# Row-wise infinity norm: early stores released one reduction sooner, and five load semaphores instead of eight

## The chip, the cores and the metric

The kernel runs on one core of a Trainium2 chip. The metric is the device time of one execution in microseconds (us); the median of several executions is quoted. The time span of a profile starts with the first instruction and is about 1.8 us shorter than the device time of the same execution. A DMA is a transfer between memory and the core; its landing is the moment when the last of its 16 completion signals has arrived, and "issue to landing" counts from the start of the instruction that issues it. A semaphore is a counter that those signals raise and that an engine can wait for.

## The reference

```python
def setup_inputs():
    return {"x": np.random.randn(8192, 8192).astype(np.float32)}

def reference(x):
    return np.linalg.norm(x, ord=np.inf, axis=1)      # max |x| of each row
```

The input is 268 MB and the output 32 KB, so nearly all of the work is to read the input once.

## The kernel before

SyncE issues all loads into a ring of three big buffers, and VectorE (DVE) reduces each piece with an absolute maximum. Most rows go in 24 loads of 16384 columns per partition, the first of the tail included. The tail (18 rows per partition) is cut into 29 pieces that get shorter towards the end, so that little is left to reduce when the last one lands. Load i may not go out before the reduction of load i-SEMS has ended, because it uses the same semaphore:

```python
SEMS = 8
...
    def load(self, at, w, src):
        i = self.started
        self.started += 1
        ins = self.nc.sync.dma_start(out=self.ring[:, at : at + w], in_=src)
        ins.then_inc(self.sems[i % SEMS], 16)
        ...
        if i >= SEMS:
            self.tc.add_manual_dep(ins.ins, self.last[i - SEMS].name, ...,
                reason="the semaphore counts one load at a time")
    def reduce(self, pairs):
        ...
        self.last.append(ins.ins)
```

The results go out in three stores: `early` (all rows of the big loads) and `middle` (16 of the 18 tail rows) from ScalarE, and `last` (the final two rows) from SyncE. The first two carry an added wait:

```python
    early = nc.scalar.dma_start(out=out[:split]..., in_=res_big...)
    middle = nc.scalar.dma_start(out=out_tail[:, : ROWS - 2], in_=res_tail[:, : ROWS - 2])
    for store in (early, middle):
        tc.add_manual_dep(store.ins, pieces.last[-2].name, ..., reason="not beside the last load")
    ...
    last = nc.sync.dma_start(out=out_tail[:, ROWS - 2 :], in_=res_tail[:, ROWS - 2 :])
```

## Time and profile before

| | before |
|---|---|
| device time, median (range) of 4 runs | 629.31 us (629.28 to 629.45) |
| span of the profile | 627.7 us |
| DVE busy | 552.1 us, 88% |
| DVE idle from 560 us to its end | none |
| last load, issue to landing | 8.85 us |
| end of DVE's work, then to the end of the span | 625.14 us, 2.54 us |

What sets the time in each stretch is worked out, with the lines, in the prediction. It was made when three of these four runs were at hand, with a median of 629.32 us.

### The profile page before, as it was taken

How to read it: one execution, taken by the hardware profiler on the slowest of the kernel's cores; microseconds unless marked ns; L12 is line 12 of the kernel's file. 1: busy time of each engine (PE TensorE's matmuls, PEld its weight loads, DVE VectorE, ACT ScalarE, POOL GpSimd, SP SyncE). 2: the span in 40 equal slices, each digit the busy share in tenths (PEclk: the TensorE clock that was granted, in tenths of full speed). 3: DMA queues.
4: the chain of work that ended last, by engine and by line, in shares of the span. 5: the costliest groups of instructions: out<-in, count | busy, mean ns of one | idle time of the engine just before them, and what ended most of it. 6: DMA issues, size and time to landing. Idle time of an engine off the chain costs nothing.

```text
span 627.7 us, 175 instructions
## 1 busy us (share of the span) xinstructions
DVE 552.1 (88%) x62; POOL 3.2 (1%) x14
## 2 busy tenths in 40 slices
DVE  0588988889988889888898888988889999999998
POOL 0000000000000000000000000000000000000000
DMA  9999999999999999999999999999999999999997
GB/s 401 405 464 405 464 405 464 405 464 401 468 401 468 401 468 401 468 401 468 401 464 405 464 405 459 409 459 409 451 407 442 425 420 438 430 434 429 423 421 296
DMA packets 7921, 268.48 MB, mean 428 GB/s; under 512 B 1264, under 2 KB 1264, under 8 KB 2416
## 3 DMA queue, kind: packets, MB, share of 16 engines
q1 hardware_dynamic: 7632, 268.44, 99.3%
q10 hardware_dynamic: 288, 0.03, 0.0%
q14 instruction: 1, 0.01, 0.0%
HBM read 268.44 MB, written 0.03 MB: 428 GB/s over the span
## 4 chain that ended last, share of the span: by engine, by line
DMA 57%; DVE 42%; issue 0%; DVEq 0%; SPq 0%
DMA ring<-in_x_dram 57%; DVE res_big L110 22%; DVE parts L110 12%; DVE res_tail L110 7%; DVE ring L110 1%; DVEq L265 0%; SPq L92 0%; DVE idle L218 0%
## 5 line engine op out<-in xcount | busy, mean ns | idle before, releaser
L110 DVE TENSOR_REDUCE res_big<-ring 128x2 f32<-128x16384 f32 x23 | 396.1, 17220 | 69.7 <-DMA ring<-in_x_dram 69.7
L110 DVE TENSOR_REDUCE parts<-ring 128x1 f32<-128x3136 f32 (+18 forms) x22 | 78.5, 3633 | 1.2 <-DMA ring<-in_x_dram 1.2
L110 DVE TENSOR_REDUCE res_tail<-ring 128x1 f32<-128x8192 f32 (+1 forms) x9 | 69.8, 7811 | 2.1 <-DMA ring<-in_x_dram 2.1
L110 DVE TENSOR_REDUCE ring<-ring 128x1 f32<-128x1600 f32 (+5 forms) x6 | 8.3, 1444 | 0.0
L207 POOL TENSOR_SCALAR res_tail<-parts 128x1 f32<-128x1 f32 x9 | 2.7, 298 | 615.9 <-DVE parts L110 615.9
L207 POOL TENSOR_SCALAR parts<-parts 128x1 f32<-128x1 f32 x1 | 0.4, 357 | 5.6 <-DVE parts L110 5.6
L254 POOL MEMSET const-uint8-127<- 128x1 uint8 x1 | 0.1, 103 | 0.0
L254 POOL MEMSET const-bfloat16-1.0<- 128x1 bf16 x1 | 0.1, 102 | 0.0
L254 POOL MEMSET const-float32-0.0<- 128x1 f32 x1 | 0.1, 99 | 0.2 <-issue 0.2
L254 POOL MEMSET const-float32-1.0<- 128x1 f32 x1 | 0.1, 99 | 0.0
L218 DVE MEMSET idle<- 1x1 f32 x2 | 0.1, 59 | 0.0
## 6 DMA issues: line engine op xcount, KB each, us to landing
ring<-in_x_dram SPq DMA_DIRECT2D x3, 4096.0 KB, 40.5
ring<-in_x_dram SPq DMA_DIRECT2D x1, 7264.0 KB, 31.1
ring<-in_x_dram SPq DMA_DIRECT2D x1, 5024.0 KB, 33.3
ring<-in_x_dram SPq DMA_DIRECT2D x1, 4544.0 KB, 34.5
ring<-in_x_dram SPq DMA_DIRECT2D x1, 4224.0 KB, 40.3
ring<-in_x_dram SPq DMA_DIRECT2D x1, 4032.0 KB, 35.5
ring<-in_x_dram SPq DMA_DIRECT2D x1, 3584.0 KB, 43.6
ring<-in_x_dram SPq DMA_DIRECT2D x2, 1568.0 KB, 39.0
```

The costliest lines, as they stand in the source:

```text
L110: ins = self.nc.vector.tensor_reduce(out=dst, in_=src, axis=mybir.AxisListType.X, op=mybir.AluOpType.max, apply_absolute_value=True,)
L207: combined = nc.gpsimd.tensor_scalar(out=to, in0=best, scalar1=two[0], scalar2=two[1] if len(two) == 2 else None, op0=mybir.AluOpType.max, ...
L218: tc.keep_in_program_order(nc.vector.memset(idle[:, i : i + 1], 0.0))
L254: nc = _bacc.Bacc("TRN2", target_bir_lowering=False, num_devices=1)
```

## The change

The intent, as the code shows it: let the early stores get out of the last store's way, without running beside the last load, and make do with fewer semaphores.

```diff
-SEMS = 8
+SEMS = 5
...
     for store in (early, middle):
         tc.add_manual_dep(
             store.ins,
-            pieces.last[-2].name,
+            pieces.last[-3].name,
```

No instruction is added or removed.

## The prediction

> **What bounds the kernel now.** I read the page first, then busy time by stage, then the chain that ended last, then the timeline of the end and the list of DMA issues. The kernel loads 268 MB and takes the largest absolute value of each row on VectorE (DVE). By stage (columns: window, its length, DVE busy, POOL busy, clock, DMA share, GB/s):
>
> ```profile
> 0.00:465.00 465.00, 395.27 (x23) 0.19 (x4) 1.00 1.00 433
> 465.00:560.00 95.00, 91.66 (x15) 0.56 (x2) 1.00 0.99 427
> 560.00:615.00 55.00, 55.00 (x16) 2.12 (x7) 1.00 1.00 424
> 615.00:625.10 10.10, 10.10 (x11) 0.36 (x1) 1.00 0.83 333
> 625.10:627.70 2.60, 0.04 (x3) 0.00 (x0) 1.00 0.11 13
> ```
>
> Up to 465 us the DMA engines are full (share 1.00, 433 GB/s) and DVE has spare time: the load bounds. From 560 us to 625.1 us DVE has no idle time at all, and the DMA engines are full too, to about 623 us: the pieces of the tail are cut so that each lands just ahead of its reduction. After 625.1 us there are 2.6 us in which only the last results are stored. The chain says the same of the end:
>
> ```profile
> 618.62 4.86 DVE ring L110 x4
> 623.48 0.06 DVE parts L110
> 623.53 0.69 issue
> 624.22 0.92 DVEq L265
> 625.14 0.00 DVE idle L218 x2
> ```
>
> It is DVE's work without a gap until 625.14 us. The timeline of the end (start, length, engine, line):
>
> ```profile
> 624.25 0.89 DVE L110 TENSOR_REDUCE res_tail<-ring 128x1 f32<-128x710 f32 x1
> 624.37 0.38 ACTq L220 DMA_DIRECT2D out_dram<-res_big  x1
> 624.51 0.36 POOL L207 TENSOR_SCALAR res_tail<-parts 128x1 f32<-128x1 f32 x1 [10.81 <-DVE parts L110]
> 624.79 0.51 ACTq L224 DMA_DIRECT2D out_dram<-res_tail  x1
> 625.08 0.06 DVE L218 MEMSET idle<- 1x1 f32 x2
> 625.16 0.35 SPq L239 DMA_DIRECT2D out_dram<-res_tail  x1
> ```
>
> The two early stores go out at 624.37 and 624.79 us, the last store at 625.16 us. The list of issues gives size and time from issue to landing:
>
> ```profile
> ring<-in_x_dram SPq DMA_DIRECT2D x1, 384.0 KB, 10.1
> ring<-in_x_dram SPq DMA_DIRECT2D x1, 352.0 KB, 8.9
> out_dram<-res_big ACTq DMA_DIRECT2D x1, 23.0 KB, 2.1
> out_dram<-res_tail ACTq DMA_DIRECT2D x1, 8.0 KB, 1.8
> out_dram<-res_tail SPq DMA_DIRECT2D x1, 1.0 KB, 1.7
> ```
>
> So the stores land at about 626.4, 626.6 and 626.8 us, the last store last, and some 0.85 us of closing instructions follow to 627.7 us. The last load was issued 8.9 us before it landed: it stood in the queue most of that time.
>
> **What the Trainium skill says.** (1) "DMA: Bandwidth & Descriptors", section "Anatomy of one DMA": a semaphore wait is made on the issuing sequencer before dispatch, and the DMA engines only consume their queues. The trace agrees: SyncE's own waits are all on reductions (456.2, 81.6 and 58.7 us for the three groups on line 92). The section also says that the fixed cost of a DMA is mostly completion latency; 1.7 us for a store of 1 KB fits. (2) Same page, "Why a DMA increments its semaphore by 16 and not by 1": one semaphore for each slot in flight. That is what SEMS is here: load i may not be issued before load i-SEMS has been reduced. (3) Same page, "Issuing engines are not separate DMA queues": DMAs of ScalarE and SyncE interleave on the same 16 engines, so early stores can get in the way of a load or of the last store. (4) "Perfetto Trace Analysis", section "Per-instruction lifecycle": descriptor generation is shared and locked for one DMA at a time. The second early store occupies 624.79 to 625.30 us, and the last store begins at 625.16 us inside that time, yet its own issue takes 0.35 us against 0.33 us of an undisturbed load issue. So at most 0.02 us of such waiting shows in the issue itself.
>
> **The change, part one: five semaphores.** It adds and removes no instruction; 52 loads and their reductions stay. What moves is the earliest issue of a load.
>
> In the first 465 us nothing moves: the ring holds three buffers of 16384 columns, so load i waits for reduction i-3 already, which is stricter than i-5. In the tail the pieces shrink (from 9088 columns to 704), more than five fit into the ring, and the wait becomes reduction i-5 in place of i-8. I worked out the tail's piece list from the kernel's planning function: the last eight pieces, loads 44 to 51, have 1600, 1472, 1344, 1152, 1024, 896, 768 and 704 columns.
>
> The last load, number 51, is the tightest. Before, it waited for reduction 43 and was issued at 615.33 us. After, it waits for reduction 46, the one of 1344 columns. That starts at 618.54 us and takes 1.55 us (list of groups by shape), so it ends at 620.10 us and the issue comes at about 620.12 us: 4.8 us later. Is that late? It needs a figure for a load that finds the queue empty. The first load of the kernel does: issued at 0.72 us, DVE released at 22.9 us, 22.1 us for 8 MiB, while consecutive loads of that size that stand in the queue land 19.3 us apart. So 22.1 - 19.3 = 2.8 us is the fixed part, as an estimate, and a cold one. The 352 KB at the 434 GB/s that 19.3 us means take 0.83 us. Even with an empty queue it would land at 620.12 + 2.8 + 0.83 = 623.75 us, and it landed at 615.33 + 8.85 = 624.18 us before. Spare time: 0.4 us. So there is still a queue ahead of it and it lands when it did.
>
> The load before it, number 50 (384 KB): reduction 45 ends at 618.62 us, so 618.64 + 2.8 + 0.91 = 622.35 us against 613.27 + 10.06 = 623.33 us; spare 1.0 us. Load 49 (448 KB): reduction 44 ends at 617.03 us, so 617.05 + 2.8 + 1.06 = 620.9 us against 610.94 + 11.42 = 622.36 us; spare 1.5 us. Farther back the pieces are larger and the spare time grows: load 40 could be issued when reduction 35 ends, 590.0 us, and landed at 605.1 us. Expected cost of part one: 0.0 us. It also gains nothing: DVE is the bound there, and a queue that is less deep moves no more bytes.
>
> **Part two: the early stores wait for the last reduction but two.** They waited for the reduction of load 50, which ends at 624.34 us (768 columns, start 623.39 us, 0.945 us); now for that of load 49 (896 columns, start 622.40 us, 1.076 us), which ends at 623.48 us. Both stores move up by 0.86 us: issues at 623.51 and 623.93 us, landings at about 625.6 and 625.8 us in place of 626.4 and 626.6 us. The last load has nearly all its bytes by then: the DMA share is 0.97 for 622 to 623 us and 0.29 for 623 to 624 us, and by the trace its last data packet ends at 623.73 us, while the first packet of an early store comes 0.88 us after its issue, thus at about 624.4 us. So the stores still do not run beside the load.
>
> What it can gain: the end is set by the last store, whose issue waits for DVE at 625.14 us, which does not move. Only its 1.67 us from issue to landing can shrink, by what the two early stores disturb it. In the trace its first packets (626.01 us) follow straight on the last packets of the second early store (626.00 us), so some disturbance is possible; but its first packet comes 0.84 us after its issue, which is no more than the 0.88 us of the first early store, which nothing disturbed. I take 0.1 us as the gain, out of a possible 0 to 0.3 us.
>
> **Sum.** 629.32 - 0.0 - 0.1 = 629.2 us.
>
> **Rivals.** (a) The queue runs dry. If the fixed part of an issue near the end is over 3.2 us in place of 2.8 us, load 51 lands late, and each 0.1 us of lateness is 0.1 us of time, because its reduction starts only 0.07 us after its landing now (624.25 against 624.18 us). In favour: 0.4 us is not much, and the 16 DMA engines do not finish together, so the fastest could run dry first. Against: first packets of the very first load came 1.0 to 1.8 us after its issue, and load 51's packets began at 621.9 us, 1.8 us after the new issue. It would give 629.5 to 630.3 us. (b) The early stores meet the last load after all. They are 31 KB together, less than 0.1 us at the rate of the loads, and small packets could make it 0.3 us; 629.3 to 629.6 us. Against: the 0.65 us between the load's last packet and the store's first. (c) The early stores were the real hold-up of the last store, through the shared descriptor generation or their writes in HBM: without them 1.67 us becomes 1.3 us and the time 628.9 us. Against: the 0.84 us above. (d) A shorter queue makes the loads themselves quicker or slower in the tail. Quicker gives nothing, since DVE has no gap there; slower would show at once. The DMA share of 1.00 in both long stages gives no reason for either.
>
> **Range and chances.** The three runs before spread by 0.17 us, and another chip or run may add as much. With (c) at the low side and (a) or (b) at the high side, 628.8 to 629.7 us should hold 8 times in 10; I give (a) one chance in ten. Two per cent would be 12.6 us; no part touches the first 465 us, and the whole end after DVE is 2.6 us. Faster 0.01, within 2% 0.98, slower 0.01.
>
> **What would show it.** Right: the early stores issue near 623.5 and 623.9 us, the last store still at 625.16 us with 1.5 to 1.7 us to landing; the last load has about 4.1 us from issue to landing in place of 8.9 us, and load 50 about 4.7 us in place of 10.1 us; DVE has no idle time from 560 us on. Wrong: a wait of DVE for the DMA of the ring near the end, or a last store that lands in under 1.4 us, or DVE's end away from 625.14 us by over 0.2 us.

## The result, and the profile after

| | before | after |
|---|---|---|
| device time, median of 4 runs | 629.31 us | 629.03 us |
| range | 629.28 to 629.45 | 628.94 to 629.06 |
| ratio | | 0.9996 (0.9981 to 1.0011) |

The ratios are from the runs of the same rounds; they can differ by up to 0.0003 from the ratio of the medians or of the means given here. The medians differ by 0.28 us, and in these eight runs the ranges do not overlap, but the stated interval includes 1.

Busy time by stage in the changed kernel (columns as in the prediction):

```profile
560.00:615.00 55.00, 55.00 (x16) 2.11 (x7) 1.00 1.00 423
615.00:624.95 9.95, 9.95 (x11) 0.36 (x1) 1.00 0.86 338
624.95:627.30 2.35, 0.03 (x3) 0.00 (x0) 1.00 0.04 1
```

DVE still has no gap from 560 us on, with five semaphores too. The stretch after DVE is shorter. The end of the changed kernel's timeline (start, length, engine, line):

```profile
623.35 0.38 ACTq L220 DMA_DIRECT2D out_dram<-res_big  x1
623.77 0.45 ACTq L224 DMA_DIRECT2D out_dram<-res_tail  x1
624.09 0.88 DVE L110 TENSOR_REDUCE res_tail<-ring 128x1 f32<-128x710 f32 x1
...
624.92 0.06 DVE L218 MEMSET idle<- 1x1 f32 x2
625.00 0.35 SPq L239 DMA_DIRECT2D out_dram<-res_tail  x1
```

The two early stores now go out 1.0 us earlier, before the last reduction starts in place of after it. The list of DMA issues of the changed kernel (size, then us from issue to landing):

```profile
ring<-in_x_dram SPq DMA_DIRECT2D x1, 384.0 KB, 4.7
ring<-in_x_dram SPq DMA_DIRECT2D x1, 352.0 KB, 4.1
out_dram<-res_big ACTq DMA_DIRECT2D x1, 23.0 KB, 1.7
out_dram<-res_tail ACTq DMA_DIRECT2D x1, 8.0 KB, 2.4
out_dram<-res_tail SPq DMA_DIRECT2D x1, 1.0 KB, 1.5
```

The last load is issued 4.1 us before it lands instead of 8.9 us, yet it lands 0.85 us after the load before it in both profiles (623.33 to 624.18 us before, 623.19 to 624.04 us after). The last store takes 1.47 us instead of 1.67 us.

The span fell by 0.39 us (627.68 to 627.29 us). The traces divide it: 0.16 us lies at the very start, where the first load landed at 22.68 us instead of 22.85 us and everything after it moved along; 0.20 us lies in the last store; 0.03 us lies in the closing instructions. In the groups of waits this start is the "longest" column of DVE's waits on the big loads (total, times, longest), first before, then after:

```profile
DVE res_big L110 <- DMA ring<-in_x_dram: 69.7, 23, 22.9
```

```profile
DVE res_big L110 <- DMA ring<-in_x_dram: 69.6, 23, 22.7
```

Nothing in the change touches the first load. So one pair of profiles cannot say whether 0.39, 0.20 or 0.0 us belongs to the change; the experiments had to.

### The profile page after: what moved, and what is told of

The parts are those of the page before. It is cut to its first block, busy times and chain, and to the rows that moved or that the text cites. A ratio compares the mean times of both kernels' runs of the same rounds, so it can differ in the third digit from the quotient of the medians.

```text
span 627.3 us, 175 instructions
## 1 busy us (share of the span) xinstructions
DVE 552.1 (88%) x62; POOL 3.2 (1%) x14
## 4 chain that ended last, share of the span: by engine, by line
DMA 57%; DVE 42%; issue 0%; DVEq 0%; SPq 0%
DMA ring<-in_x_dram 57%; DVE res_big L110 22%; DVE parts L110 12%; DVE res_tail L110 7%; DVE ring L110 1%; DVEq L265 0%; SPq L92 0%; DVE idle L218 0%
```

## The experiments

The theories were: **A**, the early stores had disturbed the last store, and moving them away gives the gain; **B**, the five semaphores give it; **C**, it is scatter between executions. (The expectation of stores_latest calls something else theory C: that stores do not disturb one another.) All runs of this section were on the same chip, each group with runs of the kernel before in its rounds. The medians of before were 629.28, 629.30 and 629.31 us in the three groups. Every kernel gave a correct result.

### The two parts apart

**after_again**: the changed kernel once more, no edit.

> The changed kernel once more. Theory A (the early stores disturbed the last store): 0.15 to 0.3 us faster than before, the last store 1.4 to 1.55 us from issue to landing. The first load's landing, which was 0.17 us earlier in the one profile of after (22.68 against 22.85 us), need not repeat, if it is chance of one execution. Theory C (all of the 0.28 us is scatter between executions): within 0.1 us of before.

Measured: 628.97 us (628.90 to 629.25, 5 runs) against 629.28 us; ratio 0.9995. The gain repeats, so theory C alone is unlikely. But its profiled execution, at 629.25 us the slowest of the five, had a last store of 1.87 us, outside the expected 1.4 to 1.55 us: two of the store's 16 completions came 0.3 us after the others. So getting the stores apart does not make the last one quick every time.

**sems5_only**:

```diff
-SEMS = 8
+SEMS = 5
```

> Five semaphores alone, early stores as before. Theory A: 0.0 us against before (within 0.1), last load about 4.1 us from issue to landing, DVE without idle time in the tail, last store again 1.6 to 1.7 us to landing. Theory B (the shorter queue or the fewer semaphores bring the gain, for instance by an earlier first landing): 0.15 to 0.3 us faster, first landing near 22.68 us.

Measured: 629.15 us (629.12 to 629.50, 5 runs); ratio 0.9999. By the means it is 0.06 us faster than before. The list of issues of this kernel:

```profile
ring<-in_x_dram SPq DMA_DIRECT2D x1, 352.0 KB, 4.1
...
out_dram<-res_tail SPq DMA_DIRECT2D x1, 1.0 KB, 2.0
```

The last load goes out as late as in the changed kernel and the last store is as slow as in the kernel before, or slower (1.99 us, above the expected 1.6 to 1.7 us). Its first landing was early too (22.49 us), and yet the time did not fall by the 0.15 us or more of theory B.

**stores_only**:

```diff
-            pieces.last[-2].name,
+            pieces.last[-3].name,
```

> Early stores one reduction earlier alone, eight semaphores. Theory A: all of the gain, 0.15 to 0.3 us faster than before, last store 1.4 to 1.55 us to landing. Theory B: within 0.1 us of before.

Measured: 629.06 us (628.93 to 629.47, 5 runs); ratio 0.9997; by the means 0.20 us faster than before. In its list of issues the last load is early again (8.9 us) and the last store quick:

```profile
ring<-in_x_dram SPq DMA_DIRECT2D x1, 352.0 KB, 8.9
...
out_dram<-res_tail SPq DMA_DIRECT2D x1, 1.0 KB, 1.4
```

This is what theory A said, but 0.20 us against a scatter of 0.2 us between single runs (standard deviation, before and here) called for a second test, below.

### How near the queue is to running dry

**sems4**:

```diff
-SEMS = 5
+SEMS = 4
```

> The changed kernel with four semaphores: the last load waits for reduction 47, at about 621.3 us, in place of reduction 46. If the fixed part of an issue with an empty queue is 2.8 us, as the first load gave it, the last load lands at about 624.9 us, and the kernel is 0.7 us slower than after, with waits of about 0.4 us before each of the last two reductions. With 2.4 us: 0.3 us slower, one wait. With 3.2 us: 1.1 us slower, three waits. If the queue never runs dry: no change.

Measured: 629.97 us (629.64 to 630.23, 5 runs), by the means 0.93 us slower than after_again in the same rounds. The profiled execution was the fastest of the five. Its timeline shows two waits of DVE, and its chain of the end now runs through the last load:

```profile
622.49 1.09 DVE L110 TENSOR_REDUCE ring<-ring 128x1 f32<-128x896 f32 x1 [0.23 <-DMA ring<-in_x_dram]
...
623.82 0.95 DVE L110 TENSOR_REDUCE parts<-ring 128x1 f32<-128x768 f32 x1 [0.24 <-DMA ring<-in_x_dram]
```

```profile
621.16 3.50 DMA ring<-in_x_dram
624.66 0.02 issue
624.69 0.89 DVE res_tail L110
```

The last load took 3.50 us from issue to landing. Less 0.83 us for its bytes, that leaves 2.67 us as its fixed part; the two loads before it, for which DVE waited, leave 2.97 and 2.98 us. That is close to the 2.8 us that the prediction took from the first load. The queue was not quite empty, though: the first packet of the last load came at 622.67 us, and packets of the load before it ran until 623.49 us. There were two waits, as expected at 2.8 us, but they came one load earlier than expected (before the reductions of loads 49 and 50) and were 0.23 and 0.24 us long in place of 0.4 us. One semaphore fewer and the tail is bound by the loads.

**sems3**:

```diff
-SEMS = 5
+SEMS = 3
```

> The changed kernel with three semaphores. The chain of load, reduction, next load closes: with a fixed part of 2.8 us the model gives the last landing at 628.1 us, 4.0 us slower than after, with DVE waiting before each of the last eight loads by 0.4 to 0.9 us; with 2.4 us 2.8 us slower; with 3.2 us 5.3 us slower.

Measured: 635.78 us (634.4 to 637.1, 4 runs); ratio to before 1.0103. That is 6.5 us slower than before by the means, more than the 4.0 us at the expected fixed part, and its runs scatter over 2.7 us. Eight reductions waited, as expected, by 0.32 to 1.06 us, but they were not the last eight: those of loads 42, 43, 45 and 47 to 51. The fixed parts of the last four loads, worked out as above, were 2.5 to 3.0 us. Loads 43 to 45, whose bytes also queue behind a load still in flight, took 3.8 to 4.5 us beyond their own transfer, which the simple model left out. The direction held, the place in part; the size was too small.

### Where the early stores may stand

**stores_latest** (both early stores wait for the last reduction):

```diff
-            pieces.last[-3].name,
+            pieces.last[-1].name,
```

> Five semaphores, both early stores wait for the last reduction itself, so that all three stores go out together near 625.0 to 625.4 us. Theory A: the stores are in each other's way, the later of them lands at 627.2 to 627.5 us, and the kernel is 0.7 to 1.0 us slower than after; the last store itself takes over 1.6 us. If stores do not disturb one another (theory C), the last store still takes about 1.5 us and only the second early store, issued some 0.4 us later, sets the end: 0.3 to 0.6 us slower than after.

Measured: 629.49 us (629.41 to 629.79, 5 runs) against 629.30 us before; some 0.5 us slower than the changed kernel of the other groups. That is the size named if stores do not disturb one another, and theory A's numbers were missed. Its timeline:

```profile
624.74 0.35 SPq L239 DMA_DIRECT2D out_dram<-res_tail  x1
624.74 0.39 ACTq L220 DMA_DIRECT2D out_dram<-res_big  x1
625.17 0.45 ACTq L224 DMA_DIRECT2D out_dram<-res_tail  x1
```

The store of the last rows went out at the same time as the first early store and was not slowed (1.49 us); the two early stores took 1.66 and 1.64 us, and the second one, issued last, set the end. Neither of these is slow: the first early store took 1.69 to 2.19 us in the five profiles with the stores one reduction earlier, and the second one 1.58 to 2.76 us in all nine profiles in which it went out at the end. So stores that start together need not slow one another, and theory A must be narrowed: it can hold only for a last store that comes behind others. In this one look the last store had none ahead of it.

**stores_m6** (the stores go out beside the last four loads):

```diff
-            pieces.last[-3].name,
+            pieces.last[-6].name,
```

> Five semaphores, both early stores wait for the last reduction but five, so that they go out near 619.9 and 620.3 us, beside the last four loads. The comment in the kernel says that this is to be avoided. If their 256 small packets and their writes hold up the loads (rival b of the prediction): a wait of DVE of 0.1 to 0.4 us for one of loads 48 to 51, and 0.1 to 0.4 us slower than after. If not: as fast as after within 0.1 us, since the last store is as much alone as there.

Measured: 629.15 us (628.91 to 629.26, 5 runs) against 629.30 us. Its timeline shows the price that the kernel's comment fears:

```profile
624.30 0.89 DVE L110 TENSOR_REDUCE res_tail<-ring 128x1 f32<-128x710 f32 x1 [0.17 <-DMA ring<-in_x_dram]
```

The last load took 4.36 us instead of 4.08 us and DVE waited 0.17 us for it. But the last store, now alone, took 1.44 us, so the kernel is not slower than before. By the means it is 0.07 us slower than after_again of the other group, less than the 0.1 us expected and within the scatter. So rival (b) is real in the trace, and its cost in time does not show.

**stores_free** (no added wait):

```diff
-    for store in (early, middle):
-        tc.add_manual_dep(
-            store.ins,
-            pieces.last[-3].name,
...
```

> Five semaphores, no added wait on the early stores: each goes out when its data is there, the first near 466 us, the second near 608 us, beside loads that have deep queues. Theory A: the last store is alone, as in after, 1.4 to 1.55 us to landing; the time is that of after within 0.1 us, unless a load in the stretch near 608 us is held up by more than its spare time of under 0.2 us before DVE, then 0.1 to 0.4 us slower.

Measured: 629.08 us (628.93 to 629.35, 5 runs); ratio 0.9997. The stores take 16.2 and 6.2 us among the loads without a gap on DVE in the tail, and the last store takes 1.44 us. By the means it is 0.07 us from after_again, as expected.

### Both factors again, in the same rounds

These four kernels are the corners of a square: stores as before or free, eight or five semaphores. The edits are those of sems5_only and stores_free, alone or together, on the kernel before.

> The kernel before against itself: ratio 1.000 within 0.0003; it measures the scatter. In its profile the first load's landing, 22.85 us in the one profile of before but 22.34 to 22.68 us in the nine others, should fall among those if it is chance of an execution; near 22.85 us if it belongs to the kernel before. The last store should again take 1.6 to 2.0 us, with its 16 completions spread over 0.4 us or more.

> Five semaphores alone, a second time. Theory A: within 0.1 us of before and of before_again. Theory B: 0.15 us or more faster than both.

> Eight semaphores, no added wait on the early stores, so that the last store is alone. Theory A: 0.2 to 0.3 us faster than before, last store near 1.44 us to landing, equal to free5_again within 0.1 us. Theory B: less gain than free5_again by 0.1 us or more.

> Five semaphores, no added wait on the early stores, a second time. Theory A: 0.2 to 0.3 us faster than before, last store near 1.44 us to landing, equal to free8.

| mean time, us (runs) | eight semaphores | five semaphores |
|---|---|---|
| stores as before | 629.21 (5) | 629.22 (4) |
| stores free | 629.06 (6) | 628.98 (5) |

The ten runs of before in these rounds had a mean of 629.28 us, so the same kernel under two names differs by 0.07 us: that is the scatter. The ratio of before_again rounds to 1.0000, as expected. Freeing the stores gains 0.15 and 0.23 us between the corners. Five semaphores change 0.0 and 0.08 us, which is about the scatter, though 0.08 us is near the 0.1 us that theory B asked for. In the profile of before_again the last store's 16 completions spread over 0.40 us, also as expected. The expected "within 0.1 us" held for sems5_again against both before and before_again. The gain of free8 over before_again, 0.15 us, is that over before, 0.22 us, less the scatter just named. The list of issues of free8 has the last store alone:

```profile
out_dram<-res_big ACTq DMA_DIRECT2D x1, 23.0 KB, 16.2
out_dram<-res_tail ACTq DMA_DIRECT2D x1, 8.0 KB, 6.2
out_dram<-res_tail SPq DMA_DIRECT2D x1, 1.0 KB, 1.4
```

The profiles put together, by what stood near the last store:

| profile | first landing | DVE's end to end of span | last store, issue to landing |
|---|---|---|---|
| before | 22.85 us | 2.54 us | 1.67 us |
| before_again | 22.48 us | 2.51 us | 1.65 us |
| sems5_only | 22.49 us | 2.83 us | 1.99 us |
| sems5_again | 22.47 us | 2.73 us | 1.46 us |
| after | 22.68 us | 2.31 us | 1.47 us |
| after_again | 22.48 us | 2.71 us | 1.87 us |
| stores_only | 22.57 us | 2.29 us | 1.43 us |
| stores_free | 22.40 us | 2.28 us | 1.44 us |
| free8 | 22.51 us | 2.31 us | 1.45 us |
| free5_again | 22.57 us | 2.30 us | 1.46 us |

The stretch after DVE has a mean of 2.65 us in the first four profiles (stores close), 2.44 us in the next three (stores one reduction earlier), and 2.30 us in the last three (stores long gone). Of the profiles that the table leaves out, sems4 and sems3 also have the stores one reduction earlier, with 2.28 and 2.26 us (the mean of that kind is then 2.37 us), and stores_m6 has them gone, with 2.28 us. In sems5_again the last store was quick, but the early store ahead of it took 2.2 us and landed 0.36 us after it, and so it set the end. A finer measure separates the kinds without exception: the median of the last store's 16 completions came 1.37 to 1.73 us after its issue in the four profiles with the stores close, and 1.31 to 1.32 us after it in all nine with the stores one reduction earlier or more. after_again is among the nine; two late completions alone made its 1.87 us. With the stores close, the packets of the second early store ended within 0.03 us of the last store's first packet, or ran beside its packets; in the nine they had ended 0.4 us or more before.

The first landing, by contrast, moves within both kinds: the 22.85 us of the first profile of before did not come again.

## Why the prediction was right

The time of 629.03 us fell inside the range, and "within 2%" was right. That says little: the range of 0.9 us also holds the unchanged kernel. The steps are the test:

- **Five semaphores cost 0.0 us.** Confirmed. The last two loads took 4.08 and 4.71 us from issue to landing (forecast: about 4.1 and 4.7 us), DVE had no gap in the tail, and sems5_only and sems5_again stayed with the repeated before. The spare time was put at 0.4 us from a fixed part of 2.8 us; sems4 measured 2.67 to 2.98 us, which by the same sum makes the spare time about 0.25 to 0.55 us, and lost 0.93 us, where 0.7 us was expected. Rival (a) was the right danger, one semaphore farther on.
- **The early stores move and do not meet the load.** Confirmed. They issued at 623.35 and 623.77 us; with the 0.16 us by which this whole execution ran earlier, these are the forecast 623.51 and 623.93 us. The first store packet, at 624.23 us, came 0.63 us after the last packet of the load. stores_m6 shows rival (b) where it does occur: 0.17 us of DVE's wait, which the quicker last store paid for.
- **A gain of 0.1 us.** The mechanism was right and the size was low. The prediction looked at the time from the last store's issue to its first packet, 0.84 us, and took that it was undisturbed. It was: it stayed at 0.85 us after the change. What shrank came after the last packet: from there to the landing it was 0.62 us before and 0.42 us after. The term measures about 0.2 us in the mean: 0.20 us in stores_only, 0.15 and 0.23 us in the square, 0.21 us in the stretch after DVE. Rival (c), in a smaller form than the 0.3 to 0.4 us named, was part of the truth. The 1.47 us in the profile of after lie just under the 1.5 to 1.7 us that were named as the sign of being right.
- **The rest of the 0.28 us** is not settled. A part of up to 0.09 us could belong to the semaphores: with the stores alike, five were faster than eight by 0.06 (sems5_only against before), 0.09 (after_again against stores_only), 0.0 and 0.08 us (the square). The same kernel differed from itself by 0.07 us, so this cannot be told from scatter. The earlier first landing in the profile of after is chance of an execution: it ranges from 22.40 to 22.85 us over the table, more than the change is worth, so a part of the first 0.28 us may be luck.

Why a store close behind another sometimes completes late was not found. It is no fixed cost: in sems5_again the last store landed after 1.46 us with close neighbours. And a landing can be late without neighbours so close, by a few of the 16 completions, as in after_again.

No kernel tried beats the changed one: free5_again, with 628.99 us against its 628.97 and 629.03 us, is the same.

## What to carry to other kernels

Where an engine works without a gap up to the end, as DVE here, a deeper load queue gained nothing that could be measured. How shallow it may get can be worked out: the issue time under the new wait, plus the fixed part of a load that finds the queue empty, plus its bytes, must lie before its old landing. After the last reduction only the last store counts, so send the other results out before it, by as much as the loads allow. Effects of 0.2 us in 629 need a repeat of the unchanged kernel and several profiles, since one execution's start can move by more.

## What the Trainium skill lacked or had wrong

- "DMA: Bandwidth & Descriptors", section "Anatomy of one DMA", gives a fixed cost of about 2.0 us for DMAs issued from GpSimd. For loads issued from SyncE the runs show more when the queue is empty or nearly so: 2.67 to 2.98 us beside the bytes of the last three loads in sems4, and 2.5 to 3.0 us for the last four loads of sems3. Part of it can be waiting behind the load before.
- The same page, section "Issuing engines are not separate DMA queues", says that DMAs of several engines interleave on the same DMA engines. It gives no figure for what that costs the completion of a small store, nor does the page's section on completion order, "Queues, rings and completion order". Here a 1 KB store that no other store had closely preceded landed after 1.44 to 1.46 us in three profiles of three, and with two stores just ahead of it after 1.46 to 1.99 us in four.
- "Perfetto Trace Analysis", section "Per-instruction lifecycle", has descriptor generation locked for one DMA at a time, with the wait for the lock inside the profiled time. In stores_latest two issues, on SyncE and ScalarE, both started at 624.74 us and took 0.35 and 0.39 us, against 0.35 and 0.38 us when they were 0.4 us or more apart. The last store's own issue took 0.35 us in every profile, so none shows that wait there. But the prediction looked at the last store's issue alone. The second early store's issue took 0.49 to 0.75 us in the four profiles in which the last store's issue began during it, against 0.44 to 0.47 us in the seven others in which it directly followed the first early store's. Whether the lock is the reason is not shown.
